# Moving weight sums, decays, a spill and filling matmuls in a fused SSD + HGRN2 decoder kernel

## The chip, the cores and the metric

One core of one Trainium2 chip runs the whole program. The metric is the device time of one execution in microseconds (us), the median of several executions. The core has five engines that take instructions in order from their own queues: TensorE (PE, matrix products), VectorE (DVE), ScalarE (ACT), GpSimd (POOL) and SyncE (SP, which here only starts transfers). DMA engines move data between HBM and the on-chip memory; POOL, SP and ACT can start such transfers.

## The reference, cut to what matters

Two layers over 512 tokens of width 1024, each a token mixer, a LayerNorm, a squared-ReLU MLP of width 4096, another LayerNorm and a small gated embedding. All values are float32.

```python
# layer 0 mixer: SSD, 32 heads of 64, state 128, chunks of 128 tokens
decay = segsum_exp(da)                  # exp(cs[l] - cs[s]) below the diagonal
y_diag = einsum(cb, decay, xdt)         # cb = C B^T by chunk
y_off  = einsum(cm, prev_state, exp(a_cs))
# layer 1 mixer: HGRN2, 8 heads of 128, chunks of 64 tokens
q, fz, v, g = split(u @ w_in, 4)
o = einsum(scores, v) + einsum(q * exp(b), s_prev)
y = rms_norm(o) * silu(g) @ w_out
# MLP, and the gate behind it
h = square(relu(x @ w1)) @ w2
```

## The kernel before, in words

**Products.** Each float32 matrix product is three matmuls of a reduced-width type (`mm3`, L119 to L122): a value is split into `hi` (a cast) and `lo` (what the cast lost), and hi·hi, hi·lo and lo·hi are added. A weight of 512 KB is loaded by SP into `raw` (three buffers), cast by ACT into `whi` (L114, six buffers) and subtracted by DVE into `wlo` (L116, six buffers). `unit` and `split` do that, and PE uses the weight some time later.

**Block products.** The large products are done by a seven-product scheme on 2x2 blocks, which needs sums and differences of weight blocks. For HGRN's v and g weights (`in_whvg`, two sets of four heads, `heads[0]` and `heads[1]`) and for the MLP gates (`in_wg`) these sums are formed ahead of time, split in hi and lo, and stored in DRAM (`pre_h`, `pre_0`, `pre_1`); `ready` reads them back. `sums_early` (L425) does it for both halves of `heads` during the SSD stage, with loads and stores started by POOL. `sums_ahead` (L391) does it for the gate during the MLP, with loads started by SP and stores by ACT. Both are generators of small steps, which the stage around them advances with `next`. `behind(x)` makes the scheduler place something after the instruction x.

**SSD stage (0 to 380 us).** The first product takes slices of x and a small weight together (`in_xw`, loads L163, casts L170 and L174). Then for pairs of heads k = 1 to 8: `decays` (L894) forms exp of the difference of running sums, 8 operations of 128x128 for each head on ACT (L907, Relu with an operand per partition, so that the exponent stays on one side) and then exp; `toks` holds these running sums, one per token, and exists once `dt_tail` has run. `mixed`, `states` and `turn_pair` hold the matmuls of the pair.

**MLP and gate (380 to 760 us).** `PERIODS` deals hidden tiles (T) and block products (Q). The gate ends with `finish` (L660): DVE multiplies (L669) and adds to `acc` (L670), the residual of 512x1024, for row chunk c and half h. After a chunk's half is final, `turn` transposes it (L624) into HGRN's input, and `mix_part` (L595) forms the block differences.

**HGRN (760 to 1000 us).** PE's order is written out by hand here. `background` gives matmuls that can fill gaps: the gated products (v and g, `gated`, ending in L1142 on DVE), q and f products (`qf`), and the output product. `JOBS` gives their order, and `GAPS` how many us of them `fill` deals after each step of `scores` and `tail`. `background` also spills `acc` to `xd` in DRAM (L1204), 2 MB in one transfer, so that its place can hold other blocks (`blocks_late`, L1147); `restore` brings it back. L1409 are the state matmuls, which need v; L1425 and L1427 the outputs, L1440 their normalisation on DVE into `qo`, L1449 their transposes.

The order of instructions on each engine follows the order of the code, shifted by priorities (`tc.high_priority(offset=...)`, where a negative offset is later); on PE it is by hand in the SSD and HGRN stages.

Of the kernel before, what the change touches and what calls it, by code (L numbers as in the profile page):

```python
# [33 lines left out]

JOBS = "q0 q1 s q2 q3 b0 q4 q5 q6 q7 b1 o".split()
LEADIN = 6.0
GAPS = (6.0, 12.0, 9.0, 9.0), (11.0, 10.0, 10.0, 10.0), (10.5, 10.5, 10.5, 10.5), (10.5, 7.0, 4.0, 3.5), (3.0, 2.0, 2.5, 0.0)
CONSTS = dict(ident=P, triu=P, eps=1, convw=96, convb=24, dskip=16, snw=16, dtc=2, hlb=8, hnw=1)
# [3 lines left out]
def trunk(ctx: ExitStack, tc, a):  # L42
# [94 lines left out]
    def project(src, xs, ps, m=P, tok=slice(0, T), hook=None, turn=None):  # L137

        hi, lo = src
        for k in range(8):  # L140
            c = slice(k * m, (k + 1) * m)
            mm3(ps[:m, tok], hi[:, c], lo[:, c], xs.h(k, tok), xs.l(k, tok), k == 0, k == 7)
            if k == hook:
                turn()


    begin("ssd")
# [243 lines left out]
    def sums_ahead(w, dst):  # L391

        for u in range(2):
            for h in range(2):
# [3 lines left out]
                with tc.high_priority(offset=LEAD):  # L398
                    for t, src in zip((w00, w01, w10, w11), (w[0][0], w[0][1], w[1][0], w[1][1])):
                        nc.sync.dma_start(t, src[u][:, cs])  # L400
                yield
# [8 lines left out]
                for pair in ((2, 3), (1, 0)), ((0, 1), (3, 2)):  # L410
                    lows = []
                    for n, t in pair:
                        x = halves_[t // 2][:, t % 2]
                        hi = tmp("sg", [P, T], F32R)
                        nc.scalar.copy(hi, f32(x))
                        nc.scalar.dma_start(dst[n, u, 0][:, cs], f32(hi))
                        with behind(marks["acc"]):
                            nc.vector.tensor_sub(x, f32(x), f32(hi))
                        lows.append((dst[n, u, 1][:, cs], f32(x)))
                    yield  # L420
                    with behind(marks["act"]):
                        for to, x in lows:
                            nc.scalar.dma_start(to, x)

    def sums_early(w, dst):  # L425

        for u in range(2):
            for h in range(2):
                cs = slice(h * 512, (h + 1) * 512)
                t = mk(b8, [P, 4, T], "b8", F32R)  # L430
                w00, w01, w10, w11 = (f32(t)[:, i] for i in range(4))
                for x, src in zip((w00, w01, w10, w11), (w[0][0], w[0][1], w[1][0], w[1][1])):
# [82 lines left out]
    def mlp_and_gate(layer, h_s, last, turns=()):  # L515
# [45 lines left out]
        wb = [[[wg[4 * j + 2 * i + u] for u in range(2)] for j in range(2)] for i in range(2)]  # L561
        ahead = sums_ahead(wb, pre)

        for g, period in enumerate(PERIODS):
# [7 lines left out]
            for n, op in enumerate(period):  # L572
# [8 lines left out]
                if 0 < g < 4 and (op == "Q" or n == 1):  # L581
                    next(ahead, None)
                if g == 4:
                    for _ in ahead:
                        pass

# [8 lines left out]
        def mix_part(h, c, v):  # L595
# [13 lines left out]
            if h:  # L609
                nc.vector.tensor_add(k1, v, k1)  # L610
                nc.vector.tensor_sub(k0, k1, k0)
                put("s2", cs, k0)
            else:
                nc.scalar.copy(k1, v)
                s3 = tmp("sg", [P, T]).rearrange("p (j t) -> p j t", j=4)
                nc.vector.tensor_sub(s3, k0, v)
                put("s3", cs, s3)
# [42 lines left out]
        def finish(c, h, sg):  # L660
# [5 lines left out]
            for i, part in enumerate(pp):  # L666
                cs = slice(i * n, (i + 1) * n)
                d = acc[:, c, h * 512 + i * n : h * 512 + (i + 1) * n]
                nc.vector.tensor_mul(sg[:, cs], part, sg[:, cs])  # L669
                (nc.vector if i == len(pp) - 1 else nc.gpsimd).tensor_add(d, sg[:, cs], d)  # L670
                if last:
# [222 lines left out]
    def decays(j):  # L894
# [9 lines left out]
        for r in range(2):  # L904
            for c in range(NCH):
                sl = slice(c * P, (c + 1) * P)
                nc.scalar.activation(  # L907
                    m[:, r, sl], csb[:, r, sl], AF.Relu, scale=-1.0, bias=cs_tok[:, c, 2 * j + r : 2 * j + r + 1]
                )
        ecs = tmp("ecs", [P, 2, 3 * P])  # L910
        nc.scalar.activation(ecs, csb[:, :, P:], AF.Exp)
        nc.scalar.activation(m, m, AF.Exp, scale=-1.0)
        nc.vector.tensor_mul(m, m, bc(cbm, 1, 2))
# [80 lines left out]

    whvg = a["whvg"]
    heads = [[[[whvg[8 * i + 4 * n + 2 * r + u] for u in range(2)] for n in range(2)] for r in range(2)] for i in range(2)]
    sums = (step for i in range(2) for step in sums_early(heads[i], a["pre_h"][i]))

    PIECES = {3: (0, 4), 4: (2, 2), 5: (0, 4), 6: (2, 2)}

    with tc.manual_schedule(engines={mybir.EngineType.PE}):
# [8 lines left out]
        for k in range(1, 9):  # L1010
# [11 lines left out]
            states(k - 1)  # L1022
            next(sums)
            decays(i - 1)
            some(mine)
            next(sums)
            if k < 8:
# [5 lines left out]
            some(theirs)  # L1033
            next(sums)
            if k == 1:
# [10 lines left out]
            if k == 2:  # L1046
                nc.sync.dma_start(acc, a["x"])
                for c in range(NCH):
                    nc.vector.tensor_scalar(acc[:, c, :], acc[:, c, :], ALPHA, None, ALU.mult)
            next(sums)  # L1050
            done = [mixed(i - 2), (mixed(i - 1))] if k != 7 else [mixed(12)]
# [7 lines left out]
            for t, d in enumerate(done):  # L1059
                finish(i - 2 + t, *d)  # L1060
            next(sums)
        some(3)
# [135 lines left out]
    def background():  # L1198
# [3 lines left out]
        for f in late:  # L1202
            f()
        nc.gpsimd.dma_start(a["xd"], acc)  # L1204
        for job in JOBS:
            i = int(job[1:] or 0)
            if job == "o":
                yield from out0()
            elif job == "s":
                blocks_late()  # L1210
            elif job[0] == "q":
                yield from qf(i)
            else:
                yield from gated(i) if i else first
# [386 lines left out]
```

## Time and profile before

| | us |
|---|---|
| median of 3 runs | 1400.86 (1400.76 to 1402.16) |
| the profiled execution | 1401.34 |
| its span | 1399.6 |
| PE busy | 1387.8 (99%) |
| DVE busy | 1104.3 (79%) |
| ACT busy | 820.5 (59%) |
| POOL busy | 62.6 (4%) |

A row of the timeline gives the start in us, the duration in us, engine, line and operation, destination and source tiles, and in brackets how long the engine was idle before it and what released it. A row of the waits gives who waited for whom, the total in us, how often, and the longest. A group's row ends in busy us and mean ns of one. A row of the windows gives the stretch, its length and then the busy us (and the number of instructions) of PE, PEld, DVE, ACT and POOL, the granted TensorE clock, the DMA share and GB/s. The granted clock is 0.999 of full speed here. DMA rows give KB of one transfer and the median us from issue to landing.

### The profile page before, as it was taken

What the parts mean: (1) busy time and instruction counts of PE and PEld (TensorE: products, weight loads), DVE (VectorE), ACT (ScalarE), POOL (GpSimd) and SP (SyncE); (2) the same over time, 40 slices, a digit from 0 to 9 for tenths busy, and PEclk for the clock granted to TensorE, in tenths of its full rate; (3) what the DMA queues carried; (4) which work ended last, traced back from release to release, by engine and by line L of the source; (5) the groups of instructions that cost most, each with busy time, mean ns of one, the idle gap of its engine ahead of it and who ended that gap; (6) DMA issues with size and microseconds to landing.
All of it is one profiled execution on the core that took longest, in us unless ns stands there. A gap on an engine that the chain in (4) does not pass through costs nothing.

```text
span 1399.6 us, 20799 instructions
## 1 busy us (share of the span) xinstructions
PE 1387.8 (99%) x7909; PEld 1159.1 (83%) x7909; DVE 1104.3 (79%) x1750; ACT 820.5 (59%) x1329; POOL 62.6 (4%) x122
## 2 busy tenths in 40 slices
PE   9999999999999999999999999999999999999998
PEld 7888888888888888888887788888898888888887
DVE  7898887788867879778888766768785887779886
ACT  6897777596455455546465355464455464555563
POOL 0121210211000000000000000000000000000000
PEclk9999999999999999999999999999999999999999
DMA  7566555554364665654384553464173656646364
GB/s 288 201 232 208 195 177 185 204 176 163 113 206 149 216 220 166 212 191 154 118 303 167 198 194 109 152 228 150 61 256 114 213 175 223 215 159 207 106 237 157
DMA packets 79252, 258.75 MB, mean 185 GB/s; under 512 B 9776, under 2 KB 10416, under 8 KB 78896
## 3 DMA queue, kind: packets, MB, share of 16 engines
q1 hardware_dynamic: 60096, 206.03, 43.9%
q0 software_dynamic: 9840, 34.61, 7.0%
q10 hardware_dynamic: 9216, 16.78, 3.3%
q8 instruction: 62, 1.02, 0.3%
q14 instruction: 38, 0.31, 0.1%
HBM read 219.57 MB, written 37.81 MB: 184 GB/s over the span
## 4 chain that ended last, share of the span: by engine, by line
PE 92%; ACT 3%; DVE 2%; DMA 1%; issue 1%; SPq 0%; DVEq 0%; ACTq 0%
PE pj L120 23%; PE pj L121 23%; PE pj L122 23%; PE py L120 5%; PE py L121 5%; PE py L122 5%; PE py L940 1%; DMA raw<-in_whq 1%; PE py L1256 1%; ACT b L907 1%; DMA a<-in_xw 1%; DVE wlo L116 1%; PE py L942 1%; PE pt L923 0%; ACT whi L114 0%
## 5 line engine op out<-in xcount | busy, mean ns | idle before, releaser
L120 PE MATMUL pj<-b,whi 128*128 128x512 f32 (+1 forms) x1000 | 380.0, 380 | 2.0 <-ACT qx L1167 1.6
L122 PE MATMUL pj<-b,wlo 128*128 128x512 f32 (+1 forms) x1000 | 377.4, 377 | 0.0
L121 PE MATMUL pj<-b,whi 128*128 128x512 f32 (+1 forms) x1000 | 377.2, 377 | 0.0
L116 DVE TENSOR_TENSOR wlo<-raw,whi 128x1024 fp32r<-128x1024 f32 x218 | 264.6, 1220 | 114.7 <-ACT whi L114 112.6
L114 ACT CAST whi<-raw 128x1024 fp32r<-128x1024 f32 x218 | 228.1, 1050 | 205.6 <-PE pj L121 79.1
L120 PEld LDWEIGHTS pj<-b,whi 128*128 128x128 f32 x1000 | 188.0, 188 | 37.4 <-ACT qx L1167 2.0
L122 PEld LDWEIGHTS pj<-b,wlo 128*128 128x128 f32 x1000 | 188.2, 188 | 34.7
L121 PEld LDWEIGHTS pj<-b,whi 128*128 128x128 f32 x1000 | 188.2, 188 | 34.0
L122 PE MATMUL pj<-whi,b 128*128 128x512 f32 (+1 forms) x482 | 187.4, 389 | 0.0
L120 PE MATMUL pj<-whi,b 128*128 128x512 f32 x448 | 176.7, 395 | 0.0
L121 PE MATMUL pj<-wlo,b 128*128 128x512 f32 x448 | 174.4, 390 | 0.0
L114 ACT CAST whi<-r 128x1024 fp32r<-128x1024 f32 x64 | 67.2, 1053 | 90.2 <-PE pj L121 67.9
L122 PEld LDWEIGHTS pj<-whi,b 128*128 128x128 f32 x482 | 90.5, 188 | 18.8 <-DVE b L1451 0.2
L120 PE MATMUL py<-whi,b 128*128 128x512 f32 x256 | 100.4, 392 | 0.0
L116 DVE TENSOR_TENSOR wlo<-r,whi 128x1024 fp32r<-128x1024 f32 x64 | 77.7, 1219 | 28.2 <-ACT whi L114 26.9
L122 PE MATMUL py<-whi,b 128*128 128x512 f32 x256 | 99.7, 389 | 0.0
L121 PE MATMUL py<-wlo,b 128*128 128x512 f32 x256 | 99.6, 389 | 0.0
L120 PEld LDWEIGHTS pj<-whi,b 128*128 128x128 f32 x448 | 84.1, 188 | 17.4 <-ACT b L1450 0.3
L121 PEld LDWEIGHTS pj<-wlo,b 128*128 128x128 f32 x448 | 84.2, 188 | 16.8
L120 PEld LDWEIGHTS py<-whi,b 128*128 128x128 f32 x256 | 48.1, 188 | 10.2 <-DVE acc L495 0.5
L122 PEld LDWEIGHTS py<-whi,b 128*128 128x128 f32 x256 | 48.0, 188 | 10.0
L121 PEld LDWEIGHTS py<-wlo,b 128*128 128x128 f32 x256 | 48.1, 188 | 9.7
(422 smaller groups left out, 2142.1 us busy)
## 6 DMA issues: line engine op xcount, KB each, us to landing
raw<-in_w SPq DMA_DIRECT2D x112, 512.0 KB, 3.8
r<-in_w SPq DMA_DIRECT2D x64, 512.0 KB, 4.1
raw<-in_wssd SPq DMA_DIRECT2D x38, 512.0 KB, 5.0
b<-in_whvg POOLq DMA_DIRECT2D x32, 256.0 KB, 6.8
a<-csd SPq DMA_DIRECT2D x16, 512.0 KB, 4.0
pre_h<-whi POOLq DMA_DIRECT2D x32, 256.0 KB, 2.5
pre_h<-b POOLq DMA_DIRECT2D x32, 256.0 KB, 3.2
raw<-in_wso SPq DMA_DIRECT2D x16, 512.0 KB, 4.3
```

The costliest lines, as they stand in the source:

```text
L114: nc.scalar.copy(hi[:, :n], f)
L116: nc.vector.tensor_sub(lo[:, :n], f, f32(hi[:, :n]))
L120: nc.tensor.matmul(out, sh, mh, start=start, stop=False, **kw)
L121: nc.tensor.matmul(out, sh, ml, start=False, stop=False, **kw)
L122: marks["pe"] = nc.tensor.matmul(out, sl, mh, start=False, stop=stop, **kw)
L907: nc.scalar.activation(m[:, r, sl], csb[:, r, sl], AF.Relu, scale=-1.0, bias=cs_tok[:, c, 2 * j + r : 2 * j + r + 1])
L940: nc.tensor.matmul(yd[64 * r : 64 * r + 64, sl], xdt[:, c, r, :], m[:, r, sl], start=True, stop=c == 0)
L942: nc.tensor.matmul(yd[64 * r : 64 * r + 64, sl], pv[:, c - 1, r, :], ecs[:, r, (c - 1) * P : c * P], start=False, stop=True,)
L1256: nc.tensor.matmul(ps[r][32 * b : 32 * b + 32, base + n * c : base + n * c + n], kk[r][:, ts], moving(r, 4 * c + b), start=True, stop=True,)
```

## The change

1. `decays`: the eight Relu operations of a head move from ACT to DVE, as one subtract and minimum with zero; the exp follows without a sign.
2. `sums_early` is called for `heads[0]` alone, with three steps for each k > 1 at lower priority. Before each round's loads POOL copies four values per partition out of `toks` into the tile that is to be loaded.
3. The sums of `heads[1]` are formed in the first MLP with `sums_ahead`, one step at each T step where no gate step is taken. `sums_ahead` starts all its loads and stores from POOL.
4. `finish` gets priority TURN for h = 1 in the first gate.
5. `acc` is spilled in four transfers: chunks 2 and 3 from `mix_part`, chunks 0 and 1 as the jobs `s0` and `s1`.
6. `GAPS` is dealt anew.

```diff
-JOBS = "q0 q1 s q2 q3 b0 q4 q5 q6 q7 b1 o".split()
+JOBS = "q0 s0 q1 s1 q2 q3 b0 q4 q5 q6 q7 b1 o".split()
-GAPS = (6.0, 12.0, 9.0, 9.0), (11.0, 10.0, 10.0, 10.0), (10.5, 10.5, 10.5, 10.5), (10.5, 7.0, 4.0, 3.5), (3.0, 2.0, 2.5, 0.0)
+GAPS = (6.0, 12.0, 10.0, 10.0), (13.0, 9.5, 9.5, 9.5), (10.0, 10.0, 10.0, 10.0), (12.5, 6.0, 4.0, 3.5), (3.0, 2.0, 2.5, 0.0)
...
@@ sums_ahead
-                        nc.sync.dma_start(t, src[u][:, cs])
+                        nc.gpsimd.dma_start(t, src[u][:, cs])
...
-                        nc.scalar.dma_start(dst[n, u, 0][:, cs], f32(hi))
+                        nc.gpsimd.dma_start(dst[n, u, 0][:, cs], f32(hi))
                         with behind(marks["acc"]):
                             nc.vector.tensor_sub(x, f32(x), f32(hi))
                         lows.append((dst[n, u, 1][:, cs], f32(x)))
+                    for to, x in lows:
+                        nc.gpsimd.dma_start(to, x)
                     yield
-                    with behind(marks["act"]):
-                        for to, x in lows:
-                            nc.scalar.dma_start(to, x)
@@ sums_early
                 t = mk(b8, [P, 4, T], "b8", F32R)
+                nc.gpsimd.tensor_copy(f32(t)[:, :, 0], toks[0][:, :, 0])
@@ mlp_and_gate
         ahead = sums_ahead(wb, pre)
+        more = sums_ahead(heads[1], a["pre_h"][1]) if turns else iter(())
...
                 if 0 < g < 4 and (op == "Q" or n == 1):
                     next(ahead, None)
+                elif 0 < g < 4:
+                    next(more, None)
@@ mix_part, h = 1
                 put("s2", cs, k0)
+                nc.gpsimd.dma_start(a["xd"][:, c], acc[:, c])
@@ finish
-                nc.vector.tensor_mul(sg[:, cs], part, sg[:, cs])
-                (nc.vector if i == len(pp) - 1 else nc.gpsimd).tensor_add(d, sg[:, cs], d)
+                with tc.high_priority(offset=0 if last or not h else TURN):
+                    nc.vector.tensor_mul(sg[:, cs], part, sg[:, cs])
+                    (nc.vector if i == len(pp) - 1 else nc.gpsimd).tensor_add(d, sg[:, cs], d)
@@ decays
-                nc.scalar.activation(
-                    m[:, r, sl], csb[:, r, sl], AF.Relu, scale=-1.0, bias=cs_tok[:, c, 2 * j + r : 2 * j + r + 1]
+                nc.vector.tensor_scalar(
+                    m[:, r, sl], csb[:, r, sl], cs_tok[:, c, 2 * j + r : 2 * j + r + 1], 0.0, ALU.subtract, ALU.min
                 )
...
-        nc.scalar.activation(m, m, AF.Exp, scale=-1.0)
+        nc.scalar.activation(m, m, AF.Exp)
@@ the SSD stage: of the five next(sums) for each k three become step(k), two go
-    sums = (step for i in range(2) for step in sums_early(heads[i], a["pre_h"][i]))
+    sums = sums_early(heads[0], a["pre_h"][0])
+
+    def step(k):
+        if k > 1:
+            with tc.high_priority(offset=-SOON):
+                next(sums, None)
@@ background
-        nc.gpsimd.dma_start(a["xd"], acc)
...
-            elif job == "s":
-                blocks_late()
+            elif job[0] == "s":
+                nc.gpsimd.dma_start(a["xd"][:, i], acc[:, i])
+                if i:
+                    blocks_late()
```

What this moves on the engines is seen in their order. First POOL's queue at the start of the program, before: right behind the constants (`cm` is a mask) stand the four loads of the first round (`b8` is the tile they fill).

```order
L189 MEMSET cm_162 128x128
L433 DMA b_83_540<-in_whvg 128x512 x4
L450 DMA pre_h<-whi_681 128x512
L451 DMA pre_h<-b_83_540 128x512
L450 DMA pre_h<-whi_681 128x512
L451 DMA pre_h<-b_83_540 128x512
```

The same place after:

```order
L192 MEMSET cm_162 128x128
L433 COPY b_130_802<-toks_455 128x4
L436 DMA b_130_802<-in_whvg 128x512 x4
L453 DMA pre_h<-whi_1081 128x512 x2
L453 DMA pre_h<-whi_1223 128x512 x2
L454 DMA pre_h<-b_130_802 128x512 x4
```

The loads now stand behind a copy that reads `toks`.

Then DVE at the end of the gate (L669 and L670 multiply and add for the last chunk halves, L628 and L603 belong to `turn` and `mix_part`, L116 to HGRN's first weights), before:

```order
L628 TENSOR_TENSOR b_1019_6133<-pt_6636,b_1017_6131 128x4x128
L603 TENSOR_TENSOR b_1057_6324<-pt_6636,b_1057_6324 128x4x128
L669 TENSOR_TENSOR sg_6627<-pj_6629,sg_6627 128x512
L116 TENSOR_TENSOR wlo_6801<-raw_6797,whi_6799 128x1024
L670 TENSOR_TENSOR acc_94<-sg_6627,acc_94 128x512
L116 TENSOR_TENSOR wlo_6834<-raw_6830,whi_6832 128x1024
```

After (L679 and L680 are the old L669 and L670, L637 and L618 and L619 the old L628, L610 and L611):

```order
L116 TENSOR_TENSOR wlo_6748<-raw_6744,whi_6746 128x1024
L601 TENSOR_TENSOR b_1104_6578<-b_1069_6340,b_1104_6578 128x4x128
L679 TENSOR_TENSOR sg_6645<-pj_6647,sg_6645 128x512
L637 TENSOR_TENSOR b_1031_6149<-pm_6619,b_1029_6147 128x4x128
L680 TENSOR_TENSOR acc_94<-sg_6645,acc_94 128x512
L618 TENSOR_TENSOR b_1069_6340<-pm_6619,b_1069_6340 128x4x128
L116 TENSOR_TENSOR wlo_6781<-raw_6777,whi_6779 128x1024
```

No L116 stands between the last multiply and its add any more.

Last, PE in HGRN before the first state matmuls (`pj` is the output of a product, the gated one ending in pj_7565 and a filling q product in pj_7600; L1256 are score blocks), before:

```order
L121 MATMUL pj_7565<-wlo_7562,b_1017_6131 128x512
L122 MATMUL pj_7565<-whi_7560,b_1019_6133 128x512
L120 MATMUL pj_7600<-b_1016_6130,whi_7596 128x512
L121 MATMUL pj_7600<-b_1018_6132,whi_7596 128x512
L122 MATMUL pj_7600<-b_1016_6130,wlo_7598 128x512
L1409 MATMUL pt_7604<-a_6674,btok_7419 128x128 x3
L1409 MATMUL pm_7605<-a_6674,btok_7420 128x128 x3
L1256 MATMUL py_1251_7620<-qo_7471,k_7019 32x56 x16
```

After, the last six of the fifteen filling matmuls (pj_7619) and what follows:

```order
L120 MATMUL pj_7619<-b_1028_6146,whi_7615 128x512
L121 MATMUL pj_7619<-b_1030_6148,whi_7615 128x512
L122 MATMUL pj_7619<-b_1028_6146,wlo_7617 128x512
L120 MATMUL pj_7619<-b_1029_6147,whi_7615 128x512
L121 MATMUL pj_7619<-b_1031_6149,whi_7615 128x512
L122 MATMUL pj_7619<-b_1029_6147,wlo_7617 128x512
L1421 MATMUL pt_7635<-a_6692,btok_7461 128x128 x3
L1421 MATMUL pm_7636<-a_6692,btok_7462 128x128 x3
L1268 MATMUL py_1263_7651<-qo_7513,k_7038 32x56 x16
```

Between the gated product and the state matmuls (now L1421) stood three filling matmuls, and now fifteen.

More of the change, by code (lines that the diff above doesn't have):

```diff
@@ L144, in project @@
                 turn()
+    whvg = a["whvg"]
+    heads = [[[[whvg[8 * i + 4 * n + 2 * r + u] for u in range(2)] for n in range(2)] for r in range(2)] for i in range(2)]
     begin("ssd")
@@ L582, in mlp_and_gate @@
                     next(ahead, None)
+                elif 0 < g < 4:
+                    next(more, None)
                 if g == 4:
                     for _ in ahead:
+                        pass
+                    for _ in more:
                         pass
@@ L993, in some @@
             next(outs)
-    whvg = a["whvg"]
-    heads = [[[[whvg[8 * i + 4 * n + 2 * r + u] for u in range(2)] for n in range(2)] for r in range(2)] for i in range(2)]
-    sums = (step for i in range(2) for step in sums_early(heads[i], a["pre_h"][i]))
+    sums = sums_early(heads[0], a["pre_h"][0])
[3 more added lines that the diff above has]
+                next(sums, None)
     PIECES = {3: (0, 4), 4: (2, 2), 5: (0, 4), 6: (2, 2)}
@@ L1022, in trunk @@
             states(k - 1)
-            next(sums)
+            step(k)
             decays(i - 1)
             some(mine)
-            next(sums)
             if k < 8:
@@ L1033, in trunk @@
             some(theirs)
-            next(sums)
+            step(k)
             if k == 1:
@@ L1049, in trunk @@
                     nc.vector.tensor_scalar(acc[:, c, :], acc[:, c, :], ALPHA, None, ALU.mult)
-            next(sums)
             done = [mixed(i - 2), (mixed(i - 1))] if k != 7 else [mixed(12)]
@@ L1060, in trunk @@
                 finish(i - 2 + t, *d)
-            next(sums)
+            step(k)
         some(3)
```

## The prediction

> **What bounds the kernel now.** I read the head of the page first: which engine is full, and which engines the chain that ended last runs through. Then the waits of TensorE (PE), since a full engine can only gain where it stands still, and after that the timelines round each wait.
>
> ```profile
> PE 1387.8 (99%) x7909; PEld 1159.1 (83%) x7909; DVE 1104.3 (79%) x1750; ACT 820.5 (59%) x1329; POOL 62.6 (4%) x122
> PE 92%; ACT 3%; DVE 2%; DMA 1%; issue 1%; SPq 0%; DVEq 0%; ACTq 0%
> PE py L120 <- ACT whi L174: 1.6, 2, 1.0
> PE pj L120 <- ACT qx L1167: 1.6, 1, 1.6
> PE pm L624 <- DVE acc L670: 1.5, 1, 1.5
> PE pt L1409 <- DVE a L1142: 1.4, 2, 0.9
> PE pj L120 <- DVE acc L246: 0.4, 1, 0.4
> ```
>
> PE is busy 1387.8 of the 1399.6 us span and is 92% of the chain. The change adds and removes no matmul, so the most it can win is about the 11.8 us in which PE is idle, plus what PE loses when it starts again after a stop. The five wait rows (us in total, times, longest) hold 6.5 us of that. Moving work between VectorE (DVE), ScalarE (ACT), POOL and the DMA queues counts only where it removes one of these waits or makes a new one. Bookkeeping: the profiled execution took 1401.34 us (span 1399.6 and 1.7 around it), 0.48 above the median of 1400.86. I work out a difference and take it from the median.
>
> **Part 1: the first weights of HGRN no longer load at the start.** This is not in the words of the change, but the order shows it: `sums_early` now begins with a POOL copy out of `toks`, and POOL's four loads of `in_whvg` stand behind it in POOL's in-order queue. They go from 1.3 us to after `toks` exists.
>
> ```profile
> 1.29 2.30 POOL L433 DMA_DIRECT2D b<-in_whvg  x4 [0.35 <-issue]
> b<-in_whvg POOLq DMA_DIRECT2D x4, 256.0 KB, 7.9
> 7.67 0.62 ACT L170 CAST b<-acc 128x512 fp32r<-128x512 f32 x1 [1.72 <-DMA acc<-in_xw]
> 10.64 0.62 ACT L170 CAST b<-acc 128x512 fp32r<-128x512 f32 x1 [2.05 <-DMA acc<-in_xw]
> 12.64 0.62 ACT L170 CAST b<-a 128x512 fp32r<-128x512 f32 x1 [1.07 <-DMA a<-in_xw]
> 13.64 0.62 ACT L170 CAST b<-b 128x512 fp32r<-128x512 f32 x1
> 7.46 0.39 PE L121 MATMUL py<-b,whi 128*128 128x512 f32 x1
> 7.69 0.39 PE L122 MATMUL py<-b,wlo 128*128 128x512 f32 x1
> 8.64 0.51 PE L120 MATMUL py<-b,whi 128*128 128x512 f32 x1 [0.57 <-ACT whi L174]
> 11.62 0.50 PE L120 MATMUL py<-b,whi 128*128 128x512 f32 x1 [1.02 <-ACT whi L174]
> 15.40 0.39 PE L120 MATMUL py<-b,whi 128*128 128x512 f32 x1
> L804 DVE COPY toks<-pm x1: 549/549/549, 46.0 to 46.0; 128x384 f32<-128x384 f32 x1
> ```
>
> Every L170 cast starts as its 384 KB slice of `in_xw` lands. While POOL's 4 x 256 KB are under way (issue at 1.3 us, median landing 7.9 us later) slices come at 7.67, 10.64 and 12.64, two to three us apart; the next comes one us later, at 13.64. One us for 384 KB is the pace of the loads alone, and POOL's 1024 KB are 2.7 slices, so without them the later slices land about 2.7 us earlier, and one a us all along. PE takes 6 matmuls for a slice, started 0.227 us apart where nothing is missing (7.46, 7.69), so 1.36 us, more than the loads need and more than ACT's 0.62 + 0.40. So it becomes the slowest. Its last matmul without a wait begins at 7.69; from 7.92 it would run three slices in 4.1 us and begin the next at 12.0 instead of 15.40: 3.4 us. Lower end: only the two idle times, 1.6. I take -3.2, near the upper end: the landings alone give 2.7, and of the 7.48 us from 7.92 to 15.40, for 4.1 us of work, what the record doesn't show as idle is slow starting after the stops, which goes with them. All later work of the SSD stage moves by the same amount, since its weight loads queue behind these slices. What POOL is now late with is read back only in HGRN, hundreds of us on; the loads then share the wires from 46 us on, where PE has no wait in the rows above.
>
> The Trainium skill ("DMA: Bandwidth & Descriptors", Issuing engines are not separate DMA queues) says that transfers started by any engine run on the same 16 engines and interleave; the landings of `in_xw` at two to three us while POOL's loads run, and one us after, agree.
>
> **Part 2: decays on DVE, half of the early sums out of the SSD stage.** 128 ACT operations of L907 become 128 DVE TENSOR_SCALARs of the same 128x128 with one operand per partition.
>
> ```profile
> L907 ACT ACTIVATE b<-a,toks 128x128 f32<-128x128 f32 x128 | 40.1, 389 | 0.4 <-PE py L940 0.3
> L787 DVE TENSOR_SCALAR xs<-xdt,ea 128x128 f32<-128x128 f32 x1 | 0.3, 282 | 0.0
> L774 DVE TENSOR_SCALAR cv<-xs 128x128 f32<-128x128 f32 x1 | 0.2, 221 | 0.0
> L449 DVE TENSOR_TENSOR b<-b,whi 128x512 fp32r<-128x512 f32 x32 | 21.2, 682 | 2.4 <-ACT whi L448 2.4
> 80.00:100.00 20.00, 20.00 (x133) 16.73 (x132) 19.66 (x30) 19.88 (x34) 3.79 (x7) 1.00 0.43 161
> 0.00:380.00 380.00, 376.83 (x2148) 315.23 (x2149) 315.86 (x475) 282.11 (x465) 53.72 (x104) 1.00 0.56 194
> ```
>
> The windows list PE, PEld, DVE, ACT, POOL busy. At 80 to 100 us DVE (19.66 of 20) and ACT (19.88) are both full, so this is where it can hurt. The two nearest rows bound a decay: 282 ns (L787, the same kind of operand) and 221 ns (L774, a constant). Operations of one kind overlap by some 0.08 us in a row (L449: 21.2/32 = 0.66 us, where back to back it is 0.60), so 0.14 to 0.28 us each, 18 to 36 us together. I take 0.20, i.e. 26 us, as L787's 282 less the overlap. What leaves: `heads[1]` means 32 DVE operations of 128x512 at about 0.60 us (19 us) and 16 ACT casts. DVE has about 7 us more work in a stage where it is busy 316 of 380; ACT has 40 + 10 us less of its 282. In the full stretch the sums also come later and with lower priority (only from k = 2 on, three steps per pair of heads instead of five), so DVE's work from the first decays to the normalised outputs at 125 us stays about equal (16 decays x 0.2 x 2 against the sums taken out), and ACT's falls. The 0.44 us wait for `acc` L246 at 125 us should go. -0.4, between -0.5 and +4 (rival 2).
>
> By the Trainium skill ("VectorE: DVE Perf Modes", Mode 2×_2P) a one-source fp32 operation in SBUF runs two elements a cycle; L774's 221 ns fits that and L787's 282, with an operand per partition, does not. By the rule the decays would be nearer 17 us than 26; the sum stays, since nothing there is on PE's path.
>
> **Part 3: the last four heads' sums in the first MLP, and all its sums' DMAs on POOL.**
>
> ```profile
> 380.00:760.00 380.00, 380.00 (x1742) 316.10 (x1741) 307.38 (x396) 208.67 (x289) 2.73 (x6) 1.00 0.57 189
> 58.66 0.54 POOL L450 DMA_DIRECT2D pre_h<-whi  x1 [55.07 <-ACT whi L448]
> pre_h<-b POOLq DMA_DIRECT2D x32, 256.0 KB, 3.2
> ```
>
> 32 x 0.60 = 19 us of DVE and 16 x 0.6 = 10 us of ACT go into 380 us in which DVE has 73 and ACT 171 free; PE has no wait there. What hides them is that slack; where it is gone for a moment, a weight's `wlo` comes up to 0.6 us later for each operation ahead of it. The 96 DMAs of the two sums (12 a round, 4 rounds each) cost POOL 0.54 us each, and it is idle there (2.73 of 380). But a sum holds one slot each of `whi` and `wlo` (6 each), and two `sg` until its store has landed (3.2 us). I take 0, between 0 and +12 (rival 1).
>
> **Part 4: the end of the first MLP and the start of HGRN.** `finish` gets priority for h = 1, and the residual is spilled in four chunks of 512 KB as they become final instead of one DMA of 2 MB.
>
> ```profile
> 760.39 1.21 DVE L116 TENSOR_TENSOR wlo<-raw,whi 128x1024 fp32r<-128x1024 f32 x1
> 761.52 0.68 DVE L670 TENSOR_TENSOR acc<-sg,acc 128x512 f32<-128x512 f32 x1
> 762.35 0.63 PE L624 MATMUL pm<-cst,acc 128*128 128x128 f32 x4 [1.46 <-DVE acc L670]
> 762.61 0.54 POOL L1204 DMA_DIRECT2D xd<-acc  x1 [32.69 <-DVE acc L670]
> xd<-acc POOLq DMA_DIRECT2D x1, 2048.0 KB, 10.9
> raw<-in_whq SPq DMA_DIRECT2D x7, 512.0 KB, 3.7
> 763.41 10.37 DMA raw<-in_whq
> 775.44 0.50 PE L120 MATMUL pj<-b,whi 128*128 128x512 f32 x1 [1.57 <-ACT qx L1167]
> ```
>
> The transposes at 762.35 wait for L670, which stands behind an L116 of 1.13 us that nobody needs yet; in the new order the last two multiply-adds stand ahead of it. The add is then due some 1.1 us sooner, and sooner still since L628 and L603 also move behind its multiply: the 1.46 us go. The second wait ends with a 512 KB load of `whq` that took 10.37 us against a median of 3.7, with 2 MB of `xd` from 762.61 to 773.5 beside it. Spread in chunks over the 15 us before, the most that is left at 763 us is the last chunk, a quarter; 512 KB more at the median pace is 2 to 4 us, so the load lands at 768 or so and the 1.57 goes too. With the restarts 3.3 us; I take -3.0. Lower end -1.5, if one of the two stays.
>
> **Part 5: HGRN's filling.** Matmuls dealt between the steps of HGRN are work that must be done anyway; their place matters only where PE waits.
>
> ```profile
> 849.16 0.71 PE L1409 MATMUL pt<-a,btok 128*128 128x128 f32 x4 [0.47 <-DVE a L1142]
> 954.61 0.71 PE L1409 MATMUL pt<-a,btok 128*128 128x128 f32 x4 [0.94 <-DVE a L1142]
> 991.17 1.13 DVE L1440 SCALAR_TENSOR_TENSOR qo<-pt,hri,b 128x128 f32<-128x128 f32 x4
> 992.49 0.60 PE L1449 MATMUL pt<-cst,qo 128*128 128x128 f32 x4
> ```
>
> The first L1409 needs values that the gated product just left; between that product and it stood 3 matmuls (0.68 us), now 15 (3.4 us): 0.47 goes. At the third there are 12 instead of 9: 0.68 of the 0.94 goes. Before the last L1449 filling falls from 22 matmuls to 14, 1.8 us less, where qo was ready about 0.2 us before PE came (991.17 + 1.13 against 992.49); but the casts of the next weights leave the way and 3 more matmuls stand ahead of L1425, so I expect it just in time; if not, up to +1.6. Together -1.1, from -1.4 to +0.5.
>
> **The sum**: -3.2 - 0.4 + 0 - 3.0 - 1.1 = -7.7, so 1393.2 us. With the good end of each term (-3.4, -0.5, -3.3, -1.4) it is -8.6, 1392.2; with start or gate half won and HGRN's end late (-1.6, +0.3, -1.5, +0.5) -2.3, 1398.5.
>
> **Rivals.** 1 (slower): POOL's one queue chokes the first MLP. Speaks for it: loads and stores of both sums now share one in-order queue, and a load that waits for a `whi` slot holds up the stores behind it; those hold `sg`, ACT's next copy waits for it, and ACT's weight casts stand behind that copy. A blocked round of 8 stores is 8 x 0.54 + 3.2 = 7.5 us; a unit of PE work is 48 x 0.227 = 10.9 us, so a round hurts only if weights run less than a unit ahead. `more` has 4 rounds. At 2.6 us each they take back 10.4 us, which is where it ends slower (-7.7 + 10.5 = +2.8, over 1403.7); at the full 7.5 us it is 1393 + 30. Against: two slots of six are lent, and loads are issued a whole step early. The Trainium skill ("DMA: Bandwidth & Descriptors", SWDGE vs HWDGE vs iDMA) adds that GpSimd's DMAs need state that DVE locks in its two-port mode, which SP's and ACT's do not; POOL's rows of 0.54 us beside a full DVE show no such delay here.
> 2: DVE becomes the bound in the SSD stage. At 0.28 us a decay its surplus is 36 - 19 = 17 us; DVE's idle time there is 64 us, but in the full stretch to 125 us, a third of the decays, hardly any. A third of 17 less what the moved sums free gives waits of 3 to 5 us: 1396 to 1398.
> 3: the start-up stays as slow (the slices are slow by themselves): 1396.4. Against it the one us pace after 12.64.
> 4: the `whq` load still waits, for a free `raw` slot rather than for the wires: +1.7, 1394.9.
> The measurement cannot tell changes within about 0.2% (2.8 us) from none.
>
> **How the numbers follow.** Forecast with its small misses (rival 4 too), 1391.0 to 1395.5: 0.60. Rivals 2 or 3, or both in part, 1395.5 to 1398.1: 0.21. Several gains eaten, by rivals 2 and 3 fully or by rounds of rival 1 worth 5 to 10 us, 1398.1 to 1403.7: 0.11. Rival 1 in full, above: 0.08. The range, 1391.0 to 1398.5, leaves out 0.18 above and next to nothing below. Faster 0.81, same 0.11, slower 0.08.
>
> **What would show it.** L170 casts at about one us from 5 us on and no `whi` L174 wait; POOL's first `in_whvg` load after 46 us; decays at 0.20 us in a row and no DVE wait of PE before 130 us; no PE wait between 380 and 760; PE at 755 to 780 without a stop, and `whq` loads at 3 to 5 us; L1421 (the old L1409) with one wait of 0.3. PE busy unchanged, DVE about 1104 + 26, ACT 820 - 40. A wait of PE on `wlo` or `whi` in the first MLP, or on `m` or `ecs` in the SSD stage, would make the prediction wrong.

## The result and the profile after

The changed kernel took 1422.85 us (median of 4 runs, 1419.74 to 1425.81) against 1401.51 for the kernel before in the same runs: a ratio of 1.0151 with a 95% interval from 1.0127 to 1.0175. It is slower by about 21 us, where 8 us faster was forecast. The profiled execution has a span of 1418.0 us, 18.4 more than before; at 1419.7 us it was the fastest of the four, 3.1 below the median.

The head of the page of the changed kernel, and its chain of work:

```profile
PE 1394.0 (98%) x7909; PEld 1160.2 (82%) x7909; DVE 1127.3 (80%) x1878; ACT 793.4 (56%) x1208; POOL 118.7 (8%) x225
PE 82%; DVE 7%; issue 4%; DMA 4%; ACT 1%; POOL 1%; SPq 0%; POOLq 0%; DVEq 0%; ACTq 0%
```

PE is idle 24.0 us instead of 11.8, and is busy 6.2 us longer for the same 7909 matmuls. DVE is busy 23 us longer and ACT 27 us less, where +26 and -40 were forecast. Of ACT's missing 13 us, 9 are table loads (the instruction ACT_TABLE_LOAD, 1.28 us each): 60 instead of 53, and 9 of them now stand at the exp of `decays`, where there were 2. DVE's share of the chain went from 2% to 7%. The waits of PE (us in total, times, longest):

```profile
PE py L120 <- DVE acc L498: 4.7, 2, 3.2
PE pj L120 <- DVE acc L249: 3.1, 1, 3.1
PE pj L122 <- DVE wlo L116: 2.6, 3, 1.1
PE pj L120 <- ACT whi L114: 2.5, 2, 1.5
PE py L121 <- DVE wlo L116: 2.3, 2, 2.0
PE pj L120 <- DVE cv L823: 1.8, 2, 1.0
PE py L120 <- ACT whi L177: 0.2, 1, 0.2
```

The old waits are gone: 1.6 us of `whi` L174 at the start is 0.2 of L177 (the same line), and `qx`, `acc` L670 and `a` L1142 no longer appear as waits of a us. New ones stand in their place: `acc` L249 and `cv` L823 in the SSD stage, and `acc` L498, `wlo` and `whi` in the first MLP, where PE never waited. The prediction had named a wait of PE on `wlo` or `whi` in the first MLP as the sign that it is wrong.

To see where it happens I take each matmul's start less the start of the one before, subtract the median of that spacing for the same pair of shapes, and add up by place. This counts idle time and slow matmuls together, for the one profiled execution of each kernel.

| us lost by PE | 0 to 20 | 20 to 380 | 380 to 700 | 700 to 780 | 780 to the end |
|---|---|---|---|---|---|
| before | 7.2 | 29.2 | -0.1 | 5.0 | 11.2 |
| after | 4.7 | 33.8 | 19.9 | 1.8 | 10.0 |
| difference | -2.5 | +4.6 | +20.0 | -3.2 | -1.2 |
| forecast | -3.2 | -0.4 | 0 | -3.0 | -1.1 |

Three of the five terms came as forecast. One was wrong by 5 us, and the one that was set to nothing is the result.

The start, after:

```profile
44.09 2.30 POOL L436 DMA_DIRECT2D b<-in_whvg  x4 [0.32 <-POOL b L433]
7.43 0.62 ACT L173 CAST b<-acc 128x512 fp32r<-128x512 f32 x1 [1.64 <-DMA acc<-in_xw]
8.42 0.62 ACT L173 CAST b<-acc 128x512 fp32r<-128x512 f32 x1
9.75 0.62 ACT L173 CAST b<-a 128x512 fp32r<-128x512 f32 x1 [0.40 <-DMA a<-in_xw]
8.41 0.50 PE L120 MATMUL py<-b,whi 128*128 128x512 f32 x1 [0.24 <-ACT whi L177]
```

POOL's loads wait until 44 us; the third to fifth slices are cast at 7.43, 8.42 and 9.75 instead of 7.67, 10.64 and 12.64, and PE stops once, for 0.24 us.

The end of the gate: the spill and the loads beside it.

```profile
xd<-acc POOLq DMA_DIRECT2D x4, 512.0 KB, 3.5
raw<-in_whq SPq DMA_DIRECT2D x5, 512.0 KB, 4.2
780.07 0.53 POOL L1220 DMA_DIRECT2D xd<-acc  x1 [2.33 <-DVE acc L680]
```

Each chunk lands in 3.5 us, the last one starts at 780 and the `whq` loads take 4.2 in the median; no `whq` load of 10 us is left up to 800 us.

The first MLP, by the windows of 470 to 700 us, before and then after (columns as above: PE, PEld, DVE, ACT, POOL busy, clock, DMA share, GB/s):

```profile
470.00:700.00 230.00, 230.00 (x1016) 190.30 (x1015) 187.02 (x236) 121.65 (x157) 1.74 (x4) 1.00 0.55 183
```

```profile
470.00:700.00 230.00, 217.09 (x929) 175.13 (x928) 186.57 (x232) 117.86 (x156) 43.49 (x81) 0.99 0.66 220
```

With more DVE work to do, DVE is busy no longer (187.0 and 186.6 of 230 us); instead PE falls from 230 to 217. In this window the second sum's work has pushed regular work out instead of filling the 43 us in which DVE is idle. That doesn't yet say that DVE's idle time is unusable. The waits of ACT in 460 to 700 us, after:

```profile
ACT whi L114 <- DMA pre_h<-whi: 13.7, 3, 6.7
ACT sg L418 <- DMA pre<-sg: 12.7, 4, 5.2
ACT whi L114 <- DMA pre<-whi: 11.9, 3, 4.2
```

ACT stands 38 us behind stores of the sums; in the kernel before it was 11.4 us (4.7 and 2.2 for `whi`, 4.5 for `sg`). The casts behind these waits are those of the weights. Such waits alone don't stop PE: without the second sum (a1 below) they are 15.7 us, and PE waits nowhere here. DVE's greatest waits in the same stretch:

```profile
DVE wlo L116 <- ACT whi L114: 21.2, 13, 4.1
DVE r L391 <- DMA r<-in_w: 7.6, 4, 5.7
```

DVE's L116 waits for the casts and its block sums for loads, and what DVE should do next stands behind them. The first row is nothing new: in the kernel before it was 27.7 us. The waits for loads of `r` grew, to 14.2 us in all from 3.6.

The first long stall of PE (waits of 1.52 and 0.96 us at 492.55 and 494.25, timeline at the end) can be followed to its start. POOL starts the loads of the second sum's second round at 480 and stores of its first up to 484, and SP loads `r` (a row of the chain gives start, length and what it is):

```profile
480.14 1.11 POOL L403 DMA_DIRECT2D whi<-in_whvg  x2
483.83 7.91 DMA r<-in_w
488.00:492.00 4.00, 3.03 (x14) 2.18 (x12) 0.17 (x1) 0.54 (x1) 0.00 (x0) 1.00 0.99 403
491.46 1.99 ACT L114 CAST whi<-raw 128x1024 fp32r<-128x1024 f32 x2 [7.95 <-issue]
491.83 1.23 DVE L391 TENSOR_TENSOR r<-r,r 128x1024 f32<-128x1024 f32 x1 [5.69 <-DMA r<-in_w]
492.98 1.22 DVE L116 TENSOR_TENSOR wlo<-raw,whi 128x1024 fp32r<-128x1024 f32 x1
```

The load takes 7.91 us (4.2 in the median) while the DMA engines are 0.99 busy. DVE stands 5.69 us in front of it, and the `wlo` that PE waits for comes behind. ACT's weight casts stop as well, for 7.95 us. The profile names no releaser, but by the trace the second sum's store out of `whi`, started at 483.04 us, lands at 491.39, after 8.35 us (5.0 in the median), which fits a slot that comes free with it. In the kernel before the DMA share from 484 to 492 us is 0.66. So a burst of transfers, in which loads and stores take long at once, is a rival to the theories below.

It is not enough by itself. The kernel before has a load of 7.9 us at 389 us without a wait of PE. In a5, the changed kernel without the second sum's DVE work, the DMA share from 484 to 492 us is 0.99 too and the load takes 8.1 us, but it starts at 481.29 instead of 483.83, and PE does not wait. In the changed kernel two DVE operations of the second sum (1.2 us, from 480.18) stand ahead of the L116 that comes before this load in the chain.

### The profile page after: what moved, and what is told of

Read it like the earlier page. It is cut to its first block, busy times and chain, and to the rows that moved or that the text cites. A ratio compares the mean times of both kernels' runs of the same rounds, so it can differ in the third digit from the quotient of the medians.

```text
span 1418.0 us, 20913 instructions
## 1 busy us (share of the span) xinstructions
PE 1394.0 (98%) x7909; PEld 1160.2 (82%) x7909; DVE 1127.3 (80%) x1878; ACT 793.4 (56%) x1208; POOL 118.7 (8%) x225
## 4 chain that ended last, share of the span: by engine, by line
PE 82%; DVE 7%; issue 4%; DMA 4%; ACT 1%; POOL 1%; SPq 0%; POOLq 0%; DVEq 0%; ACTq 0%
PE pj L120 21%; PE pj L121 21%; PE pj L122 21%; PE py L120 4%; PE py L121 4%; PE py L122 4%; DVE wlo L116 2%; DMA r<-in_w 2%; PE py L950 1%; PE py L1268 1%; PE py L952 1%; ACT whi L114 1%; DVE cv L823 1%; DMA raw<-in_wssd 0%; DMA pre<-whi 0%
## 5 line engine op out<-in xcount | busy, mean ns | idle before, releaser
L116 DVE TENSOR_TENSOR wlo<-raw,whi 128x1024 fp32r<-128x1024 f32 x218 | 265.2, 1223 | 109.7 <-ACT whi L114 108.4
L116 DVE TENSOR_TENSOR wlo<-r,whi 128x1024 fp32r<-128x1024 f32 x64 | 77.9, 1222 | 30.9 <-ACT whi L114 29.5
```

What stands on the lines that cost most here:

```text
L116: nc.vector.tensor_sub(lo[:, :n], f, f32(hi[:, :n]))
```

## The experiments

The reference for each is the kernel before in the same call, 1401.5 to 1402.5 us. I name theories after what is short: S, slots (of `whi`, `wlo`, `sg`) held until stores land; Q, POOL's one queue; D, DVE. No experiment varies the burst of transfers alone. The two columns on the right come from one profiled execution each; that of a3 took 6.3 us more than its median, that of b3 3.5 more, that of after 3.1 less.

| kernel | us | ratio to before, 95% | lost 20 to 380 | lost 380 to 700 |
|---|---|---|---|---|
| after | 1422.9 | 1.0127 to 1.0175 | 33.8 | 19.9 |
| a1, no second sum | 1401.5 | 0.9985 to 1.0004 | 37.0 | 0.1 |
| a2, transfers from SP and ACT | 1417.7 | 1.0087 to 1.0121 | 35.8 | 18.1 |
| a3, decays on ACT | 1414.9 | 1.0072 to 1.0120 | 28.7 | 26.2 |
| a4, one sum at a time | 1430.1 | 1.0183 to 1.0213 | 35.6 | 25.6 |
| a5, second sum without DVE work | 1411.8 | 1.0060 to 1.0087 | 34.8 | 11.2 |
| a6, second sum with DVE work alone | 1411.3 | 1.0052 to 1.0079 | 35.5 | 8.8 |
| a7, second sum holds slots alone | 1407.4 | 1.0023 to 1.0042 | 36.2 | 6.0 |
| a8, three sg buffers | 1422.0 | 1.0125 to 1.0152 | 34.1 | 21.8 |
| a9, second sum in a tile of its own | 1427.3 | 1.0165 to 1.0193 | 36.2 | 24.7 |
| a11, second sum at low priority | 1427.5 | 1.0166 to 1.0200 | 37.0 | 25.0 |
| a12, half of the second sum | 1410.2 | 1.0042 to 1.0072 | 34.6 | 8.8 |
| b1, before + copy from toks | 1401.0 | 0.9982 to 1.0001 | 30.0 | -0.1 |
| b2, before + spill, priority | 1398.8 | 0.9970 to 0.9988 | 29.0 | -0.2 |
| b3, before + GAPS | 1399.8 | 0.9981 to 0.9999 | 30.5 | 0.1 |
| b4, b1 + b2 + b3 | 1396.2 | 0.9945 to 0.9970 | 31.5 | -0.2 |
| b5, b4 with an earlier copy | 1400.8 | 0.9977 to 0.9995 | 35.6 | 0.1 |
| c1, before + decays on DVE | 1410.1 | 1.0033 to 1.0063 | 40.1 | 0.2 |

**Is it the second sum?** (a1)

```diff
-        more = sums_ahead(heads[1], a["pre_h"][1]) if turns else iter(())
+        more = iter(())
...
-        pre = a["pre_h"][i]
+        pre = a["pre_h"][0]
```

> The changed kernel without the sums of heads[1]: the first MLP forms only the gate's sums, and HGRN's last four heads read the stored sums of the first four. All else, the gate's sums on POOL's queue too, is as changed. Between 380 and 760 us PE lost 19.7 us more than before, by my count of the spacing of its matmuls. Theory S (the second sum holds slots of whi, wlo and sg, and what waits for them stands in front of the weights) and theory D (19 us more DVE work) both expect that loss to go, to about 1403 us, with no PE wait in 380 to 700. Theory Q (moving the sums' transfers to POOL's single queue is itself what hurts) expects 5 us or more of it to stay: 1408 or more.

1401.5 us: all 20 us of the first MLP are gone, and PE waits nowhere between 380 and 760, although the gate's sums go through POOL here too. So the queue alone does no harm in this stage; the second sum does it. The kernel still only equals the one before, since the SSD stage (37.0 against 29.2) eats what start, gate and HGRN gain.

**Is it POOL's queue, or two sums at once?** (a2: the three edits of `sums_ahead` undone; a4 as follows)

```diff
-                if 0 < g < 4 and (op == "Q" or n == 1):
-                    next(ahead, None)
-                elif 0 < g < 4:
-                    next(more, None)
+                if 0 < g < 4 and (g, n) != (1, 0):
+                    if next(ahead, more) is more:
+                        next(more, None)
```

> The changed kernel with both sums in the first MLP, but their loads started by SP and their stores by ACT, as before the change. Theory Q expects the loss in the first MLP to go: 1403 to 1406 us. Theory S, in which slots and not the queue are short, expects at most a third less: 1415 to 1423. Theory D expects no change: 1420 to 1425.

> The changed kernel with the two sums of the first MLP one after the other, a step after every unit of work, instead of both at once: the same DVE and ACT work, the same transfers on POOL, but one slot each of whi and wlo held instead of two. Theory S expects most of the loss to go: 1403 to 1409. Theory D expects the loss to stay, as DVE's work is the same: 1418 to 1424. Theory Q, the same number of transfers in one queue, expects 1410 to 1422.

With the old queues 1417.7: some 5 us of 21 less, and 18.1 of the 19.9 us by spacing stay. Q is out as the main cause; the time lies in the range of S. One sum after the other is slower still, 1430.1, above all three ranges, so it is not two sums in flight: S in that form is out. Why it is slower is not shown. The steps follow each other twice as close, and the second sum now starts at 535 us instead of 397, so that all of it lies in the later part of the stage.

**Which part of the second sum costs?** (a5 leaves out the 32 DVE operations; a6 the casts and stores; a7 both, and reads one column of each tile at the end so that the slots stay held)

> The changed kernel in which the second sum of the first MLP (heads[1]) keeps its loads, its ACT casts, its stores and the slots it holds, but leaves out its 32 DVE operations; HGRN's last four heads read the stored sums of the first four. Theory D (19 us of DVE work on an engine whose idle time can't be used): the loss of some 20 us goes but for 2 to 4 us, 1403 to 1407. Theory S (slots, stores and ACT): most of it stays, 1413 to 1422.

> The changed kernel in which the second sum keeps its loads and its 32 DVE operations, and leaves out its ACT casts and its stores; HGRN's last four heads read the stored sums of the first four. Theory D: the loss stays, 1414 to 1422. Theory S: it goes, 1403 to 1408. If both parts are needed, both this and the one without DVE work lie between, near 1408 to 1413.

```diff
+                last = tmp("hold", [P, 4])
+                with behind(marks["acc"]):
+                    for i, t in enumerate((w00, w01, w10, w11)):
+                        nc.vector.tensor_copy(last[:, i : i + 1], t[:, 0:1])
```

> The changed kernel in which the second sum only loads its weights and holds its slots of whi and wlo for four steps, until four copies of one column on DVE; its sums, casts and stores are left out, and HGRN's last four heads read the stored sums of the first four. Without the second sum at all it took 1401.5 us, without its DVE work 1411.8, without its casts and stores 1411.3, with all 1422.9. If the two halves are the DVE work and the casts with the stores, slots and loads alone cost little: 1402 to 1405. If the slots (theory S) are what both halves share, 1408 to 1412.

1411.8, 1411.3 and 1407.4, over 1401.5 without the sum: 10.3, 9.8 and 5.9. So loads and held slots cost 5.9, DVE's work 4 more, casts and stores 4 more, and the last 7 of the 21.4 us appear only when all is there. a5 and a6 came where they were expected if both parts are needed; D alone and S alone missed, and a7 came between its two ranges.

By place these are not the same stalls added up: a7 loses 5.5 us and a6 7.4 between 660 and 680 us, a5 only 2.0 there. And DVE's idle time was not useless in itself. From 460 to 700 us DVE is busy in a6, which has the second sum's DVE work without its casts and stores, 204.8 us, against 195.0 in a1:

```profile
460.00:700.00 240.00, 240.00 (x1060) 198.56 (x1059) 195.01 (x246) 126.24 (x165) 24.35 (x45) 1.00 0.56 184
460.00:700.00 240.00, 236.00 (x1021) 192.94 (x1020) 204.76 (x259) 118.89 (x151) 30.97 (x57) 0.99 0.59 195
```

PE was idle 4.0 us of the first MLP in a6 and 3.7 in a7, hardly a difference, but 8.5 in a5 and 12.9 with everything.

**Can one shortage be relieved?** (a8 sets `sg=3`; a9 gives the second sum a tile of `b8`; a11 lowers its priority)

> The changed kernel with three sg buffers instead of two in the MLPs; nothing is left out. If ACT standing behind copies that wait for a store to leave sg is the main part of the half that casts and stores cost (some 10 us), this gives 4 us or more: 1419 or less. If it is the whi and wlo slots waiting for stores, or ACT's own work, 1420 to 1424.

> The changed kernel in which the second sum works in a tile of its own (one of the nine 16 KB-wide b8 buffers) and holds no slot of whi and wlo; its DVE work, casts, stores and loads all stay, and nothing is left out. Holding the slots alone cost 5.9 us (1407.4 against 1401.5). If the slots are also what makes DVE work and stores cost more together than apart (21.4 for all, 5.9 + 4.0 + 4.4 by the single steps), this takes off 6 to 13 us: 1410 to 1417. If DVE's work and the stores alone do that, 1417 to 1422. If b8 itself is short, it is slower than 1423.

```diff
-                halves_ = [mk(p, [P, 2, T], tag, F32R) for p, tag in ((whip, "whi"), (wlop, "wlo"))]
+                four = mk(b8, [P, 4, T], "b8", F32R)
+                halves_ = [four[:, 0:2], four[:, 2:4]]
```

> The changed kernel with the second sum's instructions at lower priority than the weights' (by the same TURN that finish gets), nothing left out. If its DVE and ACT work costs because it stands ahead of weights and of acc in in-order queues, and there is idle time further on that can be used, the loss of 21 us falls by a third or more: 1416 or less. If no usable idle time is left on DVE, the order does not matter: 1419 to 1426.

```diff
-                    next(more, None)
+                    with tc.high_priority(offset=-TURN):
+                        next(more, None)
```

None helps: 1422.0, 1427.3, 1427.5. With all six slots back (a9) PE's greatest wait is that for DVE's addition of a block product:

```profile
PE py L120 <- DVE acc L532: 10.5, 2, 5.6
```

a8 came as expected if the `sg` slots are not the main part. a9 came where its expectation says that `b8` itself is short, and the trace agrees: ACT's block cast (L358) stands 13.8 us behind stores that leave `b8`. So a9 cannot tell whether held slots couple the parts; the stall between 480 and 500 us, at least, is gone in it. a11 shows that a later place in the queues does not help; an earlier one was not tried.

**Does it grow with the amount?** (a12: `for u in range(1)` in the second sum)

> The changed kernel with half of the second sum (two of its four rounds, all in the first two thirds of the stage); HGRN's last four heads read the stored sums of the first four. If each us of DVE work adds a us, 1411 to 1413 (half of 21.4 over 1401.5). If the loss comes from the dense end of the stage, 640 to 700 us, where the changed kernel lost 8.5 us, 1403 to 1408.

1410.2: 8.7 us for half the work, between the two ranges. By spacing 7.7 of the 8.8 us lie between 480 and 500 us, and nothing after 640, so the dense end of the stage is not what makes it dear here. But it is one stall, that of the second round, and up to 3.4 us of it are half clock (6.8 us at a granted clock of 0.50). The first round, whose loads start at 397 us, cost nothing. So near half the loss for half the work is in part luck, and a price of a us of time for a us of DVE work is not shown; the changed kernel loses 5.9 us in that stall and 8.5 between 640 and 700 us.

**The SSD stage.** (a3 and c1 swap the eight operations of `decays`, which one call does for two heads, 128 in all, and the sign of the exp; c1 does it to the kernel before)

> The changed kernel with the decays back on ACT (128 Relu operations), the sums of heads[0] in the SSD stage as changed. The SSD stage lost 4.5 us more than before (waits at 120, 124 and 213 us for DVE's cv and acc). If the 29 us of decays on DVE cause it, these waits go and the time falls by 4 to 5 us, to about 1418; if it is the later place of the early sums, the waits stay: 1422.

> The kernel before with one part of the change: the decays as 128 TENSOR_SCALARs on DVE. DVE gets 29 us more work in the SSD stage and all early sums stay there. If DVE's place in the full stretch up to 125 us is the bound, PE waits there for cv and acc as in the changed kernel or longer: 1406 to 1412 beside 1402. If ACT's relief makes up for it: 1401 to 1403.

With the decays back on ACT the stage loses 28.7 us instead of 33.8, the waits for `cv` are gone and that for `acc` is 0.2 us, and the run takes 8 us less by the medians, more than expected (its profiled execution was slower, with 26.2 us lost in the first MLP). The decays are thus shown to be what this stage loses by. In the kernel before, the decays on DVE alone cost 7.8 us, and the waits name the convolution, which stands behind them on DVE:

```profile
PE pj L120 <- DVE cv L813: 7.2, 3, 4.5
```

That is net of ACT's relief of some 40 us. Taking half of the sums out of this stage gave back only a part. The 33.8 us of the changed kernel are the least of eleven kernels with this same SSD stage, which lose 33.8 to 37.0.

**The parts that gained.** b1 has the copy out of `toks`, b2 the spill and the priority, b3 GAPS, b4 all of them on the kernel before; b5 copies from the constants instead:

```diff
-                nc.gpsimd.tensor_copy(f32(t)[:, :, 0], toks[0][:, :, 0])
+                nc.gpsimd.tensor_copy(f32(t)[:, :, 0], ident[:, 0:4])
```

> The kernel before with one line of the change: POOL copies four values out of toks ahead of each round's loads in sums_early, so that the first loads of in_whvg start after 43 us instead of at 1.3. The start gained 2.5 us in the changed kernel. If those loads held up in_xw, this gives -2.5 to -3.2 us, 1399 beside 1402; if the sums, now 40 us late, press on DVE or ACT in the full stretch to 125 us, a part comes back: 1400 to 1402.

> The kernel before with the spill in four chunks and the priority in finish alone. In the changed kernel PE lost 3.1 us less between 700 and 780 us: 1399 beside 1402.3. If the whq load still waits, 1400.7.

> The kernel before with the new GAPS alone. HGRN's loss of 10.4 us by the spacing of PE's matmuls was 8.5 in the changed kernel: -1.3 to -1.8, about 1400.8 beside 1402.3.

> The kernel before with the parts whose stages gained: the copy ahead of the loads in sums_early, the residual spilled in four chunks, the priority in finish, the new GAPS. Sums and decays stay where they were before. By the stages of the changed kernel the start gives -2.5, the end of the gate -3.1, HGRN -1.8, together -7.4: about 1395 beside 1402.5. If the gains hang on the parts left out, 1398 to 1402.

> The kernel before with the spill in chunks, the priority in finish, the new GAPS, and the copy ahead of the early loads out of the constants (which land at about 13 us) instead of toks (43 us). With toks this kernel took 1396.2, and the SSD stage gave back 2.3 of the 3.0 us that the start gained, by the spacing of PE's matmuls. If the late sums cause that, starting them at 13 us keeps the whole gain: 1393.5 to 1395. If the loads now press on the first in_wssd weights, 1396 to 1398.

b2 gives 2.8 us and b3 1.8, near what was expected. b1 gives 3.1 by spacing at the start, but only 1.0 in the medians (an interval that just includes nothing), since the stage behind loses 0.8 and the rest is within what the runs vary. b4, 1396.2, beats both kernels: 5.7 us less than the one before, where 7.4 were expected; it is what b1, b2 and b3 give together (5.6). b5, 1400.8, is slower than both of its ranges, and shows that the loads are not free: started at 13.7 us they miss the first slices, but DVE's first sum operation (L437) then stands in its queue ahead of the convolution's and waits 7.91 us for them.

```profile
13.71 2.30 POOL L434 DMA_DIRECT2D b<-in_whvg  x4 [0.32 <-POOL b L431]
26.89 0.69 DVE L437 TENSOR_TENSOR b<-b 128x512 f32<-128x512 f32 x1 [7.91 <-DMA b<-in_whvg]
33.93 0.79 PE L120 MATMUL pj<-b,whi 128*128 128x512 f32 x1 [3.90 <-ACT whi L114]
```

The start stays as good (4.6 us lost), and PE then stands 3.9 us for a weight at 34 us.

## Why the prediction was wrong

The step that failed is part 3. Its term was set to 0 within 0 and +12 with the sentence that DVE has 73 and ACT 171 us free and that "what hides them is that slack". It measured +20, and without the second sum 0.1 (a1). Two things were wrong in that step. It set only the DVE and ACT work against the slack, and left loads, stores and held slots to the upper end and to rival 1, at nothing in the forecast; but without any DVE work the second sum still costs 10.3 us (a5), and its loads and slots alone 5.9 (a7). And it counted idle time from a share of busy time over 380 us, where it should have been asked what each idle piece of DVE was waiting for. At the first long stall DVE stands 5.69 us in front of a load, and all that comes behind it in the queue waits too; in b5 it is 7.91 us. Some of the slack was real: in a6 DVE was busy 9.8 us longer than in a1, at some 4 us above the cost of loads and slots.

Rival 1 had the right place and sign, with a chance of 0.08. That its full price, 1393 + 30, meets the measured 1422.9 us is luck, since its mechanism was at most a part: POOL's queue is some 5 us of 21 (a2), and a third `sg` buffer changes nothing beyond the spread of the runs (a8). What stays open is which shortage couples the parts, so that 7 us appear only with all of them together. At the first long stall three things come together: a burst of transfers, a slot held by a store, and a load that starts later behind DVE work. The other stalls were not followed in the same way, and no single edit removed the loss.

Part 2 failed by size: -0.4 with an upper end of +4, and +4.6 came. The decays' price was right:

```profile
L917 DVE TENSOR_SCALAR b<-a,toks 128x128 f32<-128x128 f32 x128 | 28.9, 285 | 3.5 <-PE py L950 3.5
```

28.9 us against the forecast 26, 0.23 a piece, and 0.196 from start to start in a row. What was wrong is the sentence that DVE's work up to 125 us "stays about equal". It counted 32 decays, and 48 run before the addition to `acc` that PE waits for; from the end of `toks` to that addition DVE is busy 79.2 us, where it was 73.7. PE waits 3.1 us for `acc` at 127 us, and 0.8 and 1.0 for `cv` at 121 and 215, and c1 gives 7.8 us for the decays without the sums' departure: rival 2, with the price of its upper end. The rule of the Trainium skill ("VectorE: DVE Perf Modes", Mode 2×_2P) of two elements a cycle does not describe these operations: 285 ns, like L787's 282 with an operand per partition, and not L774's 221.

The upper end of the range, 1398.5, was added up with +0.3 and 0 for parts 2 and 3, though their own upper ends were +4 and +12.

Part 1 was right in mechanism and a little large (-2.5 for -3.2 in the changed kernel, -3.1 in b1): the slices do not come one a us all along, as the third is still cast 2.6 us after the second. Behind it a cost was missed, because the deferred loads and sums were priced at nothing (the SSD stage of b4 loses 2.3 us more than that of the kernel before). Part 4 (-3.2 for -3.0; b2 -2.8) and part 5 (-1.2 for -1.1; b3 -1.8) held. The last L1449 came in time, as chosen.

## What to carry to other kernels

Free time of an engine with an in-order queue is not by itself a place to put work. Before moving work onto an engine beside a full one, list what ends each of its idle pieces in that stage, and ask whether it is the chain that feeds the full engine. Price the transfers and the buffers that come with the work too: here they cost about as much as the work. Waits of the full engine that have one visible cause (a burst of transfers, an instruction ahead in a queue) were predicted to within 0.7 us each; the big error lay in the part for which the profile showed no wait at all.

## What the hardware did that I had not expected

After some waits PE runs at half speed for about 3 us. The timeline of PE after, and the windows with the granted clock (the number before the DMA share):

```profile
492.55 0.50 PE L120 MATMUL pj<-b,whi 128*128 128x512 f32 x1 [1.52 <-ACT whi L114]
494.25 0.79 PE L122 MATMUL pj<-b,wlo 128*128 128x512 f32 x1 [0.96 <-DVE wlo L116]
495.27 0.63 PE L121 MATMUL pj<-b,whi 128*128 128x512 f32 x1
495.69 0.63 PE L122 MATMUL pj<-b,wlo 128*128 128x512 f32 x1
497.40 0.39 PE L120 MATMUL pj<-b,whi 128*128 128x512 f32 x1
497.63 0.39 PE L121 MATMUL pj<-b,whi 128*128 128x512 f32 x1
```

```profile
494.00:496.00 2.00, 1.75 (x4) 1.46 (x5) 2.00 (x3) 1.40 (x2) 0.00 (x0) 0.50 0.40 102
498.00:500.00 2.00, 2.00 (x11) 1.63 (x10) 2.00 (x4) 0.89 (x1) 0.00 (x0) 1.00 0.84 285
```

Matmuls start 0.42 us apart at a granted clock of 0.50, and 0.23 apart again from 497.4 on. So 2.5 us of waiting cost some 2 us more. The clock is granted at 0.50 a second time in this stage, from 688.5 us on, behind a wait of 3.2 us; behind a wait of 2.0 us at 611 and one of 1.6 at 671 it is not. Between 380 and 700 us PE was idle 12.9 us and lost 19.9: of the rest, 7 us, 3.3 are slow clock (two stretches of 3.4 us) and the others slow starts after the stops. They show as busy time of PE, which is 6.2 us longer in all. The Trainium skill ("TensorE: Matmul & The Clock Gate", Part 1: The HAM clock gate) describes a gate that passes half the pulses until the array has been busy for some 3.4 us; the 3.2 us of slow matmuls here, from 494.25 to 497.40, agree. A wait of PE can thus be worth more than its length.
